# A fused 3x3 convolution and 2x2 max pool: a written-out issue order for its first and last steps, seven weight blocks from six vector operations, three row differences on GpSimd, the last step in halves

## The chip, the cores and the metric

The kernel runs on one core of one Trainium2 chip. The metric is the device time of one execution in microseconds (us). Engines are called PE (TensorE), DVE (VectorE), ACT (ScalarE), POOL (GpSimd) and SP (SyncE, which issues most DMAs here).

## The reference

```python
x = np.random.randn(16, 64, 64, 64)          # batch, channels in, height, width
weight = np.random.randn(128, 64, 3, 3) * 0.1
x_pad = np.pad(x, ((0, 0), (0, 0), (1, 1), (1, 1)))
conv[b, co] += weight[co, ci, kh, kw] * x_pad[b, ci, kh:kh+h, kw:kw+w]   # over ci, kh, kw
output[b, c, i, j] = np.max(conv[b, c, 2*i:2*i+2, 2*j:2*j+2])           # 16 x 128 x 32 x 32
```

## The kernel before, in words

Two images at a time stand on the 128 partitions (64 channels each). The 16 images are eight such pairs. Pairs alternate between two ways of computing: "k" pairs, whose input is a bf16 tile `kx`, and "w" pairs, whose input is an fp32 tile `wx`. A pair's 32 output rows are cut into 4 quarters of 8 rows. One **step** i (0 to 15) handles one quarter of one k pair and the same quarter of one w pair.

The pooling maximum over two neighbouring rows is taken before all products are added: max(a + c, b + c) = max(a, b) + c. So a step builds two PSUM accumulators for the k quarter and two for the w quarter. Each accumulator is a tile of 128 x 2 x 8 x 64 fp32 (the two images side by side); there are four in PSUM. The pieces of a step, with the names that the text uses (upper case for k, lower case for w; the kernel before has the same pieces as functions):

- **PA**: 12 matmuls (`pa`) into the first k accumulator, with weight blocks D2 and G0. **EV** (`evac`): ACT copies it to SBUF.
- **PB**: 12 matmuls (`pb`) into the second k accumulator, with blocks D0 and G2. **MX** (`rowmax`): DVE takes the maximum of it and the copy. **PR**: 6 matmuls (`pr`) add the common part, block G1 times `ks`.
- **OD** (`odd`): ACT copies the odd columns. **CM** (`colmax`): DVE takes the maximum of even and odd columns into `o`, and SP sends `o` out.
- **P2**: 6 matmuls (`p2`) into the first w accumulator, block GM times `we`. **SE** (`se`): ACT writes its negative into the second one. **P0** and **P3** (6 matmuls each) add products of row differences to the first and to the second. **ev**, **mx**, **P1** (6 matmuls, GP times `ws`), **od** and **cm** then do for w what EV, MX, PR, OD and CM do for k.
- The row sums and differences: **KS** (`prep_ks`, bf16) and **WS** (`prep_ws`, fp32) run on DVE, **E** (`prep_we`) on POOL (on DVE for step 0). **Z** (`prep_wz`) is one POOL operation that takes differences two rows apart for all 16 rows of a quarter; P0 reads its even rows and P3 its odd rows.

A step is thus 54 matmuls, all from the helper `taps` (line 159): 864 in all. The 64-partition halves of the array work on the two images at the same time.

Before the steps the weights are loaded (`wraw`), combined into eight blocks `wq` of three kernel columns each (D2 = g2 - g1, D0 = g0 - g1, G0, G1, G2, NG2 = -g2, GM and GP = (g0 + g2 -/+ g1) / 2), transposed on PE (`turn`) and copied back to `wt`. The first rows of the first k pair come as fp32 (`kfirst`) and are cast on DVE in two halves, odd rows (line 301) and even rows (line 311). All other `kx` rows come by DMAs that POOL issues (`kload`), all `wx` rows by DMAs of SP (`wload`). `dummy` issues matmuls on zeros.

The program's order is fixed by hand (`manual_schedule`): each engine takes its instructions in the order in which the code issues them. Lines 291 to 332 are the head; the loop at line 343 issues the pieces of step i mixed with those of step i - 1. `behind(a, b)` makes POOL operation `a` wait for DVE operation `b`:

```python
def behind(inst, other):
    tc.add_manual_dep(inst.ins, other.ins.name, SYNC, reason="shared SBUF port")
...
if i == 0:
    behind(prep_we(1, nc.gpsimd), prep_ws(0))
    prep_wz(1)
preps(i + 1)
```

Of the kernel before, what the change touches and what calls it, by code (L numbers as in the profile page):

```python
# [11 lines left out]
def kernel(  # L12
# [19 lines left out]

    nc = tc.nc
# [5 lines left out]
    MULT = mybir.AluOpType.mult  # L39
# [9 lines left out]
    LEADW = 4  # L49
# [23 lines left out]


# [6 lines left out]
    kfirst = const.tile([128, 2 * R + 1, W], FP32, name="kfirst")  # L81
    nc.sync.dma_start(out=kfirst, in_=rows_of(0, *chunk(0)))

    def kload(j, lo, hi):
        if j not in kx:
            kx[j] = kx_pool.tile([128, H, W], BF16, name="kx")
        nc.gpsimd.dma_start(out=kx[j][:, lo:hi, :], in_=rows_of(2 * j, lo, hi))  # L87
# [5 lines left out]

    for i in range(LEADW):
        wload(i)
# [5 lines left out]
    kload(0, *chunk(1))  # L101
# [5 lines left out]
    D2, G0, D0, G2, GM, NG2, G1, GP = range(0, 24, 3)  # L107
    wv = wraw.rearrange("a (ci k) -> a k ci", k=K * K)
    g0, g1, g2 = wv[:, 0:3, :], wv[:, 3:6, :], wv[:, 6:9, :]
    wq = const.tile([CO, 26, CI], BF16)  # L110
    wt = const.tile([128, 25, CO], BF16)
    nc.vector.memset(wq[:, 0, :], 0.0)
    nc.vector.memset(wq[:, 25, :], 0.0)
    gsum = const.tile([CO, 3, CI], FP32)
    ghalf = const.tile([CO, 3, CI], FP32)

    def dummy(n, tiles):
        for i in range(n):
            yt = tiles[(i // 2) % len(tiles)]
            nc.tensor.matmul(  # L120
                yt[:, i % 2], zeros[:, 0:128], zeros, start=True, stop=True, skip_group_check=True
            )

    tbank = [acc[t][:, h] for t in (1, 2, 2, 3) for h in range(2)]
    tcount = [0]

    def slots(m):
        return wq[:, m + 1 : m + 4, :]  # L130

    def turn(m, engine):
        tp = tbank[tcount[0]].rearrange("p a b -> p (a b)").bitcast(BF16)
        tcount[0] += 1
        n = 4 if m == GP else 3
        for j in range(n):
            nc.tensor.transpose(  # L137
                tp[:, j * 128 : (j + 1) * 128],
                wq[:, m + j : m + j + 2, :].rearrange("a b c -> a (b c)"),
                ident,  # L140
            )
        dst = wt[:, m : m + n, :].rearrange("p a b -> p (a b)")
        if engine is nc.scalar:
            nc.scalar.copy(out=dst, in_=tp[:, 0 : n * 128])  # L144
        else:
            engine.tensor_copy(out=dst, in_=tp[:, 0 : n * 128])  # L146


    def taps(dst, m0, rows, start=False, skip=None):
        for kw in (1, 0, 2):  # L150
            i0, i1 = 0, R
            if skip == 0:
                i0 = 1
            if skip == R - 1:
                i1 = R - 1
            o0, o1, c0, c1 = (0, W, 0, W) if kw == 1 else (1, W, 0, W - 1) if kw == 0 else (0, W - 1, 1, W)
            for half in range(2):
                lo = half * CI
                nc.tensor.matmul(  # L159
                    dst[:, half, i0:i1, o0:o1],  # L160
                    wt[lo : lo + CI, m0 + kw + 1 - half, :],
                    rows(lo, i0, i1, c0, c1),
                    start=start and kw == 1,
                    stop=True,
                    skip_group_check=True,
                )

    def step1(t, first):
# [7 lines left out]


    SYNC = mybir.DependencyInfo(mybir.DependencyClass.Sync, mybir.DependencyReason.DATA)

    def behind(inst, other):  # L180
        tc.add_manual_dep(inst.ins, other.ins.name, SYNC, reason="shared SBUF port")

    ks, ws, we, wz = {}, {}, {}, {}

    def prep_ks(i):
        j, q = divmod(i, NQ)
        if q == 0:
            ks[j] = ks_pool.tile([128, HO, W], BF16, name="ks")
        v = kx[j][:, 2 * R * q : 2 * R * (q + 1), :]
        return nc.vector.tensor_tensor(  # L190
            out=ks[j][:, q * R : (q + 1) * R, :], in0=v[:, 0::2, :], in1=v[:, 1::2, :], op=ADD
        )

    def prep_ws(i):
        j, q = divmod(i, NQ)
        if q == 0:
            ws[j] = ws_pool.tile([128, HO, W], BF16, name="ws")
        v = wx[j % 2][:, 1 + 2 * R * q : 1 + 2 * R * (q + 1), :]
        return nc.vector.tensor_tensor(  # L199
            out=ws[j][:, q * R : (q + 1) * R, :], in0=v[:, 0::2, :], in1=v[:, 1::2, :], op=ADD  # L200
        )

    def prep_we(i, engine):
        j, q = divmod(i, NQ)
        if q == 0:
            we[j] = we_pool.tile([128, HO, W], BF16, name="we")
        v = wx[j % 2][:, 1 + 2 * R * q : 1 + 2 * R * (q + 1), :]
        return engine.tensor_tensor(  # L208
            out=we[j][:, q * R : (q + 1) * R, :], in0=v[:, 1::2, :], in1=v[:, 0::2, :], op=SUB
        )  # L210

    def prep_wz(i):
        j, q = divmod(i, NQ)
        if q == 0:
            wz[j] = wz_pool.tile([128, H, W], BF16, name="wz")
        a = 2 * R * q
        return nc.gpsimd.tensor_tensor(  # L217
            out=wz[j][:, a : a + 2 * R, :],
            in0=wx[j % 2][:, a : a + 2 * R, :],
            in1=wx[j % 2][:, a + 2 : a + 2 * R + 2, :],  # L220
            op=SUB,
        )
# [24 lines left out]
    def se(i):
        tb["w", i] = free.popleft()
        nc.scalar.mul(tb["w", i], ta["w", i], -1.0)  # L249

    def p0(i):
        j, q = divmod(i, NQ)
        taps(ta["w", i], G0, step2(wz[j], 2 * q * R))

    def p3(i):
        j, q = divmod(i, NQ)
        taps(tb["w", i], NG2, step2(wz[j], 2 * q * R + 1))

    def p1(i):
        j, q = divmod(i, NQ)  # L260
        taps(tb["w", i], GP, step1(ws[j], q * R))

    def evac(*g):
        ev[g] = ev_pool.tile([128, 2, R, W], FP32, name="ev")
        nc.scalar.copy(out=ev[g], in_=ta[g])  # L265
        free.append(ta.pop(g))

    def rowmax(*g):
        t = tb[g]
        nc.vector.tensor_tensor(out=t, in0=t, in1=ev.pop(g), op=MAX)  # L270

    def odd(*g):
        od[g] = od_pool.tile([128, 2, R, WO], FP32, name="od")
        nc.scalar.copy(out=od[g], in_=tb[g][:, :, :, 1::2])  # L274

    def colmax(*g):
        t = tb.pop(g)
        o = o_pool.tile([128, 2, R, WO], FP32, name="o")
        nc.vector.tensor_tensor(out=o, in0=t[:, :, :, 0::2], in1=od.pop(g), op=MAX)  # L279
        free.append(t)  # L280
        j, q = divmod(g[1], NQ)
        p = 2 * j + (g[0] == "w")
        nc.sync.dma_start(
            out=out[2 * p : 2 * p + 2, :, q * R : (q + 1) * R, :].rearrange(
# [3 lines left out]
        )  # L288


    dummy(8, [acc[1], acc[2], acc[0], acc[3]])
    klo, khi = chunk(0)
    nc.vector.tensor_sub(out=slots(D2), in0=g2, in1=g1)
    nc.scalar.copy(out=slots(G0), in_=g0)
    nc.vector.tensor_sub(out=slots(D0), in0=g0, in1=g1)
    nc.scalar.copy(out=slots(G2), in_=g2)
    turn(D2, nc.vector)
    turn(G0, nc.scalar)
    turn(D0, nc.vector)
    nc.scalar.mul(ghalf, g1, 0.5)  # L300
    nc.vector.tensor_copy(out=kx[0][:, 1:khi:2, :], in_=kfirst[:, 1:khi:2, :])  # L301
    turn(G2, nc.scalar)
    dummy(2, [acc[0]])
    nc.vector.tensor_add(out=gsum, in0=g0, in1=g2)
    nc.scalar.mul(slots(NG2), g2, -1.0)
    nc.vector.scalar_tensor_tensor(
# [109 lines left out]
```

## Time and profile before

| | us |
|---|---|
| median of 3 timed runs (lowest, highest) | 119.13 (117.88, 120.91) |
| the profiled execution: its own time | 118.08 |
| its span, first to last instruction | 116.3 |
| PE, DVE, ACT, POOL busy | 101.9, 84.7, 72.6, 61.6 |
| mean granted TensorE clock | 0.972 |

The span is 1.8 us shorter than the time of the same execution; all positions in the text are microseconds from the span's start. A busy PE only says that matmuls were under way, so the text counts matmuls and the idle time between them. "Idle before, releaser" in a row is the time the engine stood still, and what ended it.

### The profile page before, as it was taken

The page shows a single profiled execution, that of the slowest core. Times are in us where ns is not written, and L with a number is a line of the kernel's source. Part 1 is how long each engine was busy: PE and PEld are TensorE (multiplying, and loading weights), DVE is VectorE, ACT ScalarE, POOL GpSimd, SP SyncE. Part 2 cuts the span into 40 slices and gives each one's busy share as a digit, 9 for nine tenths or more (in the row PEclk, how much of TensorE's full clock was granted, in tenths as well). Part 3 has the DMA queues.
Part 4 walks back from the last instruction along what each step waited for, and adds up shares of the span by engine and source line. Part 5 has one row for each costly group of instructions (what it writes and reads, how often), then busy time and mean ns, then how long its engine had stood idle before and what let it go on. Part 6 is the DMA issues. An engine that isn't in the chain of part 4 may idle for free.

```text
span 116.3 us, 2320 instructions
## 1 busy us (share of the span) xinstructions
PE 101.9 (88%) x901; PEld 49.3 (42%) x901; DVE 84.7 (73%) x111; ACT 72.6 (62%) x90; POOL 61.6 (53%) x49
## 2 busy tenths in 40 slices
PE   5787974699999999999999999999999999999120
PEld 2333331245455554544555445454554545455000
DVE  1464799758787878787878787878787878787520
ACT  4465338036768676767686767676867676768320
POOL 6000499855656585856386767663965656500000
PEclk9999999679999999999999999999999999999995
DMA  3999129988869488999894799997949422222222
GB/s 99 280 314 368 44 27 186 231 201 145 255 225 208 162 204 146 229 262 253 311 263 148 217 149 263 217 272 286 269 145 208 152 85 93 90 98 88 99 81 90
DMA packets 12459, 21.70 MB, mean 187 GB/s; under 512 B 928, under 2 KB 9120, under 8 KB 12448
## 3 DMA queue, kind: packets, MB, share of 16 engines
q1 hardware_dynamic: 11296, 17.63, 46.9%
q0 software_dynamic: 1152, 3.92, 21.7%
q8 instruction: 7, 0.11, 0.5%
q14 instruction: 4, 0.03, 0.1%
HBM read 17.07 MB, written 8.39 MB: 219 GB/s over the span
## 4 chain that ended last, share of the span: by engine, by line
PE 79%; DVE 10%; DMA 5%; ACT 1%; issue 1%; SPq 0%; DVEq 0%
PE acc L159 78%; DVE ws L199 5%; DMA kfirst<-in_x_dram 5%; DVE acc L270 2%; DVE o L279 1%; PE acc L137 1%; ACT od L274 1%; DVE wt L146 1%; DVE ks L190 1%; ACT wt L144 0%; DVE kx L301 0%; SPq L69 0%; DVEq L146 0%
## 5 line engine op out<-in xcount | busy, mean ns | idle before, releaser
L159 PEld LDWEIGHTS <-wt 64*128 64x128 bf16 x864 | 46.5, 95 | 54.7 <-issue 10.0
L159 PE MATMUL acc<-kx,wt 64*128 64x504 bf16 (+3 forms) x384 | 47.7, 381 | 2.9 <-DVE o L279 2.6
L270 DVE TENSOR_TENSOR acc<-acc,ev 128x1024 f32<-128x1024 f32 x32 | 39.3, 1227 | 13.1 <-PE acc L159 13.1
L217 POOL TENSOR_TENSOR wz<-wx 128x1024 bf16<-128x1024 f32 x16 | 37.7, 2354 | 10.7 <-DVE ks L190 10.7
L265 ACT COPY ev<-acc 128x1024 f32<-128x1024 f32 x32 | 32.4, 1013 | 12.6 <-PE acc L159 11.7
L208 POOL TENSOR_TENSOR we<-wx 128x512 bf16<-128x512 f32 x15 | 19.1, 1272 | 27.5 <-DVE ws L199 21.4
L274 ACT COPY od<-acc 128x512 f32<-128x512 f32 x32 | 18.7, 585 | 19.3 <-PE acc L159 19.3
L279 DVE TENSOR_TENSOR o<-acc,od 128x512 f32<-128x512 f32 x32 | 22.1, 691 | 7.5 <-ACT od L274 7.5
L159 PE MATMUL acc<-wz,wt 64*128 64x504 bf16 (+1 forms) x192 | 23.6, 377 | 0.7 <-POOL wz L217 0.7
L249 ACT ACTIVATE acc<-acc 128x1024 f32<-128x1024 f32 x16 | 16.1, 1008 | 2.2 <-PE acc L120 1.8
L199 DVE TENSOR_TENSOR ws<-wx 128x512 bf16<-128x512 f32 x16 | 16.0, 997 | 0.0
L159 PE MATMUL acc<-ws,wt 64*128 64x504 bf16 (+1 forms) x96 | 13.4, 382 | 2.5 <-DVE acc L270 2.5
L159 PE MATMUL acc<-we,wt 64*128 64x504 bf16 (+1 forms) x96 | 13.2, 377 | 0.2 <-POOL we L208 0.2
L159 PE MATMUL acc<-ks,wt 64*128 64x504 bf16 (+1 forms) x96 | 13.2, 377 | 0.0
L190 DVE TENSOR_TENSOR ks<-kx 128x512 bf16<-128x512 bf16 x16 | 6.6, 414 | 0.0
L120 PE MATMUL acc<-zeros 128*128 128x512 bf16 x12 | 4.5, 517 | 1.2 <-DVE zeros L98 1.2
L87 POOL DMA_DIRECT2D kx<-in_x_dram x8 | 4.7, 584 | 0.1
L137 PE MATMUL acc<-ident,wq 128*128 128x128 bf16 x25 | 2.6, 219 | 2.0 <-DVE wt L146 1.4
L146 DVE COPY wt<-acc 128x384 bf16<-128x384 bf16 (+1 forms) x4 | 1.5, 374 | 3.4 <-PE acc L137 3.4
L144 ACT COPY wt<-acc 128x384 bf16<-128x384 bf16 x4 | 1.9, 478 | 2.9 <-PE acc L137 2.9
L137 PEld LDWEIGHTS <-wq 128*128 128x128 bf16 x25 | 1.6, 97 | 3.7 <-issue 2.9
L120 PEld LDWEIGHTS <-zeros 128*128 128x128 bf16 x12 | 1.3, 126 | 3.3 <-issue 2.1
(25 smaller groups left out, 9.8 us busy)
## 6 DMA issues: line engine op xcount, KB each, us to landing
out_dram<-o SPq DMA_DIRECT2D x32, 256.0 KB, 3.4
wx<-in_x_dram SPq DMA_DIRECT2D x8, 512.0 KB, 6.8
wx<-in_x_dram SPq DMA_DIRECT2D x4, 544.0 KB, 8.9
kx<-in_x_dram POOLq DMA_DIRECT2D x4, 496.0 KB, 8.0
wx<-in_x_dram SPq DMA_DIRECT2D x4, 480.0 KB, 4.8
kx<-in_x_dram POOLq DMA_DIRECT2D x3, 528.0 KB, 9.1
kfirst<-in_x_dram SPq DMA_DIRECT2D x1, 544.0 KB, 5.4
wraw<-in_weight_dram SPq DMA_DIRECT2D x1, 288.0 KB, 3.0
```

The source lines that it names most:

```text
L120: nc.tensor.matmul(yt[:, i % 2], zeros[:, 0:128], zeros, start=True, stop=True, skip_group_check=True)
L137: nc.tensor.transpose(tp[:, j * 128 : (j + 1) * 128], wq[:, m + j : m + j + 2, :].rearrange("a b c -> a (b c)"), ident,)
L159: nc.tensor.matmul(dst[:, half, i0:i1, o0:o1], wt[lo : lo + CI, m0 + kw + 1 - half, :], rows(lo, i0, i1, c0, c1), start=start and kw == 1, ...
L190: return nc.vector.tensor_tensor(out=ks[j][:, q * R : (q + 1) * R, :], in0=v[:, 0::2, :], in1=v[:, 1::2, :], op=ADD)
L199: return nc.vector.tensor_tensor(out=ws[j][:, q * R : (q + 1) * R, :], in0=v[:, 0::2, :], in1=v[:, 1::2, :], op=ADD)
L208: return engine.tensor_tensor(out=we[j][:, q * R : (q + 1) * R, :], in0=v[:, 1::2, :], in1=v[:, 0::2, :], op=SUB)
L217: return nc.gpsimd.tensor_tensor(out=wz[j][:, a : a + 2 * R, :], in0=wx[j % 2][:, a : a + 2 * R, :], in1=wx[j % 2][:, a + 2 : a + 2 * R + ...
L249: nc.scalar.mul(tb["w", i], ta["w", i], -1.0)
L265: nc.scalar.copy(out=ev[g], in_=ta[g])
L270: nc.vector.tensor_tensor(out=t, in0=t, in1=ev.pop(g), op=MAX)
L274: nc.scalar.copy(out=od[g], in_=tb[g][:, :, :, 1::2])
L279: nc.vector.tensor_tensor(out=o, in0=t[:, :, :, 0::2], in1=od.pop(g), op=MAX)
```

## The change

Six things change. (1) The order of all pieces is written out as a list of names: `HEAD` (steps 0 to 3), `STEADY` (steps 4 to 12, the same order each time) and `TAIL` (steps 13 to 15). (2) Seven weight blocks take the place of eight: NG2 goes, and the halving of GM and GP moves into the copies out of PSUM. One ACT copy writes G0, G1 and G2; D2, D0, GM, GP are DVE operations and g0 + g2 one on POOL; each takes its elements in another order than before. (3) Z is split: `wz` for P0 and `wy` (**Y**) for P3, each 8 rows, so that a step has three POOL operations of 128 x 512 elements in place of one of that size and one of twice that. Every POOL operation waits for the last DVE operation on SBUF tiles that the list names before it. (4) The four zero matmuls in the head outside the warm-up of eight go; two are issued where the first SE needs a PSUM tile in a defined state. (5) The first `kload` waits for the sixth warm-up matmul; the later ones are issued behind Y.0, and behind Y of the third and fourth quarter. (6) EV, MX, ev, mx, OD, CM, od and cm of step 15 are done for one image at a time (".0", ".1"), and their output goes out in four DMAs of half the size.

```diff
-    D2, G0, D0, G2, GM, NG2, G1, GP = range(0, 24, 3)
+    G0, G1, G2, D2, D0, GM, GP = 1, 4, 7, 11, 15, 19, 23
...
+    def on_vector(inst):
+        sbuf_op[0] = inst
+        return inst
+    def on_gpsimd(inst):
+        behind(inst, sbuf_op[0])
+        return inst
...
+    def turn_out(m):
...
+        if m == "GM":
+            nc.scalar.mul(dst, src, 0.5)
+        elif m == "GP":
+            nc.vector.tensor_scalar_mul(out=dst, in0=src, scalar1=0.5)
...
-        taps(tb["w", i], NG2, step2(wz[j], 2 * q * R + 1))
+        taps(tb["w", i], G2, step1(row["wy", i // NQ], i % NQ))
...
+    def wz(i):
+        on_gpsimd(row_op(nc.gpsimd, "wz", i, -1, 1, SUB))
+    def wy(i):
+        on_gpsimd(row_op(nc.gpsimd, "wy", i, 2, 0, SUB))
+        j, q = divmod(i, NQ)
+        if i == 0:
+            kload(0, chunk(2)[0], H)
+        if q == 2 and j + 1 < NP // 2:
+            kload(j + 1, 0, H // 2 + 1)
+        if q == 3 and j + 1 < NP // 2:
+            kload(j + 1, H // 2 + 1, H)
...
+    def kernel_rows():
+        nc.scalar.copy(out=wq[:, G0 : G0 + 9, :].rearrange("a k c -> a c k"), in_=wv)
...
+    HEAD = """
+        D2 D0 GS TD2 VD2 GA TG0 VG0 TG1 VG1 TG2 VG2 TD0 XE GM TGM GP TGP XO KS.0 VD0 VGM VGP
+        PA.0 EV.0 Y.0 PB.0 E.0 P2.0 SE.0 MX.0 PA.1 EV.1 PR.0 Z.0 P0.0 P3.0 E.1 WS.0 P2.1 KS.1
+        OD.0 CM.0 PB.1 Z.1 ev.0 WS.2 SE.1 P0.1 ev.1 mx.0 P1.0 od.0 Y.1 P3.1 MX.1 PR.1 OD.1 PA.2
+        E.2 WS.1 KS.2 cm.0 PB.2 CM.1 P2.2 Z.2 mx.1 P1.1 EV.2 MX.2 PR.2 SE.2 od.1 cm.1 OD.2 CM.2
+        Y.2 E.3 Z.3 Y.3 P0.2 P3.2 KS.3 WS.3 PA.3 E.4 ev.2 mx.2 P2.3 EV.3 Z.4 PB.3 SE.3 Y.4 MX.3
+        P1.2 od.2 cm.2 P0.3 P3.3 ev.3 PR.3 KS.4 WS.4
+    """
+    STEADY = """
+        PA+0 OD-1 E+1 CM-1 P2+0 mx-1 EV+0 Z+1 PB+0 SE+0 Y+1 P1-1 MX+0 P0+0 od-1 P3+0 cm-1 ev+0
+        PR+0 KS+1 WS+1
+    """
+    TAIL = """
...
+        mx.14 Y.15 Z.15 EV.15.0 EV.15.1 PB.15 MX.15.1 MX.15.0 SE.15 P0.15 P3.15 ev.15.0 mx.15.0
+        ev.15.1 mx.15.1 P1.14 od.14 cm.14 PR.15 OD.15.1 OD.15.0 CM.15.0 CM.15.1 P1.15 od.15.0
+        cm.15.0 od.15.1 cm.15.1
+    """
...
+    for n in range(8):
+        warm = zero(n // 2, n % 2)
+        if n == 5:
+            behind(kload(0, *chunk(1)), warm)
```

In `HEAD`, "T" before a block's name is its transposes, "V" its copy out of PSUM; GA is `kernel_rows`, GS is g0 + g2 on POOL, XE and XO are the casts of even and odd rows of `kfirst`.

What this does to the instruction order at three places. First DVE in the head, from the second cast on, before (`acc_88` to `acc_90` are PSUM accumulators; line 146 copies a transposed block out of PSUM, 208 is E, 190 KS, 270 MX, 199 WS, 279 CM):

```order
L311 CAST kx<-kfirst 128x9x64
L146 COPY wt<-acc_89 128x384
L314 SCALAR_TENSOR_TENSOR wq<-gsum,ghalf 128x192
L208 TENSOR_TENSOR we<-wx_93 128x512
L146 COPY wt<-acc_90 128x512
L190 TENSOR_TENSOR ks<-kx 128x512
L270 TENSOR_TENSOR acc_88<-acc_88,ev 128x1024
L199 TENSOR_TENSOR ws<-wx_93 128x512
L190 TENSOR_TENSOR ks<-kx 128x512
L199 TENSOR_TENSOR ws<-wx_93 128x512
L279 TENSOR_TENSOR o<-acc_88,od 128x512
L270 TENSOR_TENSOR acc_90<-acc_90,ev 128x1024
```

The same place on DVE after the change (line 335 is a cast, 354 and 357 are GM and GP, 247 is every row sum or difference, 166 and 162 copy out of PSUM, 298 is MX, 317 CM):

```order
L335 CAST kx<-kfirst 128x9x64
L354 TENSOR_TENSOR wq<-gsum,wraw 128x64x3
L357 TENSOR_TENSOR wq<-gsum,wraw 128x64x3
L335 CAST kx<-kfirst 128x8x64
L247 TENSOR_TENSOR ks<-kx 128x512
L166 COPY wt<-acc_78 128x512
L162 TENSOR_SCALAR wt<-acc_80 128x512
L247 TENSOR_TENSOR we<-wx_82 128x512
L298 TENSOR_TENSOR acc_78<-acc_78,ev 128x1024
L247 TENSOR_TENSOR ws<-wx_82 128x512
L247 TENSOR_TENSOR ks<-kx 128x512
L317 TENSOR_TENSOR o<-acc_78,od 128x512
```

The second WS no longer stands between KS.1 and the first CM; GM and GP now stand between the two casts, ahead of the odd rows that PA.0 reads.

Second, POOL in the head, before (217 is Z, 87 issues a `kx` load):

```order
L217 TENSOR_TENSOR wz<-wx_93 128x1024
L87 DMA kx<-in_x_dram 128x1984
L87 DMA kx<-in_x_dram 128x2112
L208 TENSOR_TENSOR we<-wx_93 128x512
L217 TENSOR_TENSOR wz<-wx_93 128x1024
```

and after (345 is GS, 95 issues a `kx` load):

```order
L95 DMA kx<-in_x_dram 128x1024
L345 TENSOR_TENSOR gsum<-wraw 128x64x3
L247 TENSOR_TENSOR wy<-wx_82 128x512
L95 DMA kx<-in_x_dram 128x1984
L247 TENSOR_TENSOR wz<-wx_82 128x512
L247 TENSOR_TENSOR we<-wx_82 128x512
```

The first difference of step 0 moved ahead of the load of the later rows, and one load for the second k pair left this place.

Third, the end of DVE's program, before:

```order
L279 TENSOR_TENSOR o<-acc_88,od 128x512
L270 TENSOR_TENSOR acc_90<-acc_90,ev 128x1024
L270 TENSOR_TENSOR acc_88<-acc_88,ev 128x1024
L279 TENSOR_TENSOR o<-acc_90,od 128x512
L279 TENSOR_TENSOR o<-acc_88,od 128x512
L270 TENSOR_TENSOR acc_87<-acc_87,ev 128x1024
L279 TENSOR_TENSOR o<-acc_87,od 128x512
```

and after:

```order
L298 TENSOR_TENSOR acc_81<-acc_81,ev 128x1024
L298 TENSOR_TENSOR acc_78<-acc_78,ev 128x512 x2
L298 TENSOR_TENSOR acc_79<-acc_79,ev 128x512 x2
L317 TENSOR_TENSOR o<-acc_81,od 128x512
L317 TENSOR_TENSOR o<-acc_78,od 128x256 x2
L317 TENSOR_TENSOR o<-acc_79,od 128x256 x2
```

The last mx (on `acc_87` before, on `acc_79` after) stood behind CM.15 and stands ahead of it now, in two halves.

388 lines of the change are left out of this document (179 added, 209 removed).

## The prediction

> **What bounds the kernel now.** I read the shares of the chain that ended last first, then that chain in order of time, then the two places where it leaves PE. The shares by engine:
>
> ```profile
> PE 79%; DVE 10%; DMA 5%; ACT 1%; issue 1%; SPq 0%; DVEq 0%
> ```
>
> PE carries it, so the question is where PE is not fed. The chain (start, length, what):
>
> ```profile
> 1.19 5.44 DMA kfirst<-in_x_dram
> ...
> 6.65 0.44 DVE kx L301
> ...
> 7.13 1.39 PE acc L159 x12
> ...
> 14.28 1.90 DVE ws L199
> 16.18 0.34 DVE ks L190
> 16.51 4.33 DVE ws L199
> 20.84 0.61 DVE o L279
> ...
> 21.49 86.67 PE acc L159 x792
> ...
> 109.41 1.23 DVE acc L270
> ...
> 110.69 0.84 PE acc L159 x6
> ...
> 111.55 0.59 ACT od L274
> ...
> 112.16 0.69 DVE o L279
> ```
>
> There are three parts. From 7.13 to 21.49 the chain runs over DVE (WS, KS, WS, CM); of the 864 matmuls only 864 - 792 - 6 = 66 are done by then. From 21.49 to 108.16 PE runs 792 without a hole. Then it waits 2.5 us for mx, runs the last 6 and leaves copy, maximum and write to the end. The middle is PE's own rate, as one matmul group of two successive steps shows (PA.5 and PA.6):
>
> ```profile
> 44.19 1.47 PE L159 MATMUL acc<-kx,wt 64*128 64x512 bf16 x12
> ...
> 50.02 1.47 PE L159 MATMUL acc<-kx,wt 64*128 64x512 bf16 x12
> ```
>
> 5.83 us for 54 matmuls is 0.108 us each, and 864 of them take **93.3 us**. The first tap starts at 7.13 and the last ends at 111.53, so holes in between are 111.53 - 7.13 - 93.3 = **11.1 us**. From 111.53 to the end of the span are 4.8 us: 1.3 of copy and maximum, 3.45 of the last write from 112.85 on. The kernel after has the same 864 taps of the same shapes, so I predict three things: when the first tap starts, the holes, and the end.
>
> **Why there are holes.** DVE and POOL in the worst stretch, and PE behind it:
>
> ```profile
> 16.44 4.41 DVE L199 TENSOR_TENSOR ws<-wx 128x512 bf16<-128x512 f32 x1
> 16.69 1.29 POOL L208 TENSOR_TENSOR we<-wx 128x512 bf16<-128x512 f32 x1
> ...
> 17.92 2.36 POOL L217 TENSOR_TENSOR wz<-wx 128x1024 bf16<-128x1024 f32 x1
> ...
> 21.49 2.74 PE L159 MATMUL acc<-kx,wt 64*128 64x512 bf16 x12 [2.63 <-DVE o L279]
> ```
>
> The view of the tile `ws` has the durations of WS (least, median, most, in ns):
>
> ```profile
> L199 DVE TENSOR_TENSOR ws<-wx x16: 682/683/4405, 14.2 to 102.0; 128x512 bf16<-128x512 f32 x16
> ```
>
> A WS that takes 0.68 at its median takes 4.41 and ends 0.6 us after POOL's two operations: it makes no way while POOL reads the same SBUF. CM.0 stands behind it, PB.1 waits for CM.0's accumulator. The stall also cost the clock (columns: window, length, busy PE, PEld, DVE, ACT, POOL, granted clock, DMA share, GB/s):
>
> ```profile
> 21.00:22.00 1.00, 0.51 (x4) 0.25 (x5) 1.00 (x2) 0.00 (x0) 1.00 (x1) 0.54 1.06 215
> 22.00:23.00 1.00, 1.00 (x8) 0.39 (x6) 0.58 (x1) 0.00 (x0) 1.00 (x2) 0.50 0.94 246
> ...
> 24.00:25.00 1.00, 1.00 (x10) 0.52 (x8) 0.67 (x1) 0.00 (x0) 1.00 (x2) 0.76 0.85 231
> ```
>
> After 2.6 us without matmuls (18.9 to 21.5) PE runs at half clock until about 24.5, some 1.5 us of work lost (the 12 taps at 21.49 took 2.74, against 1.47).
>
> **The change part by part.** Durations that I use:
>
> ```profile
> L270 DVE TENSOR_TENSOR acc<-acc,ev 128x1024 f32<-128x1024 f32 x32 | 39.3, 1227 | 13.1 <-PE acc L159 13.1
> L217 POOL TENSOR_TENSOR wz<-wx 128x1024 bf16<-128x1024 f32 x16 | 37.7, 2354 | 10.7 <-DVE ks L190 10.7
> ...
> L208 POOL TENSOR_TENSOR we<-wx 128x512 bf16<-128x512 f32 x15 | 19.1, 1272 | 27.5 <-DVE ws L199 21.4
> ...
> L279 DVE TENSOR_TENSOR o<-acc,od 128x512 f32<-128x512 f32 x32 | 22.1, 691 | 7.5 <-ACT od L274 7.5
> ...
> L190 DVE TENSOR_TENSOR ks<-kx 128x512 bf16<-128x512 bf16 x16 | 6.6, 414 | 0.0
> ...
> L87 POOL DMA_DIRECT2D kx<-in_x_dram x8 | 4.7, 584 | 0.1
> ...
> L296 ACT CAST wq<-wraw 128x192 bf16<-128x192 f32 x1 | 0.5, 533 | 0.0
> ...
> L293 DVE TENSOR_TENSOR wq<-wraw 128x192 bf16<-128x192 f32 x1 | 0.5, 501 | 2.6 <-DMA wraw<-in_weight_dram 2.6
> ...
> L311 DVE CAST kx<-kfirst 128x576 bf16<-128x576 f32 x1 | 0.5, 484 | 0.0
> L301 DVE CAST kx<-kfirst 128x512 bf16<-128x512 f32 x1 | 0.4, 428 | 0.6 <-DMA kfirst<-in_x_dram 0.6
> ...
> L306 DVE SCALAR_TENSOR_TENSOR wq<-gsum,ghalf 128x192 bf16<-128x192 f32 x1 | 0.4, 359 | 0.1
> ```
>
> *First tap, later by 1.3 us.* PA.0 now needs XE, GM, GP and XO behind each other on DVE, from `kfirst` landing at 6.6 (chain above): 0.48 + 0.50 + 0.50 + 0.43, less about 0.05 overlap at each start, ends at 8.4; PA.0 starts at 8.45 instead of 7.13. GM and GP in the new element order are not in the trace. Below, 0.36 each (line 306, contiguous); above, 0.68 (a WS of 512 elements), so -0.3 to +0.35; I take line 293, which also reads strided weights. The other head operations have cover. GA on ACT costs between 0.53 (one block, line 296) and three times that, from 3.8 on; PE needs it only before TGM at 7.6, so even 1.6 is hidden under the wait for `kfirst`. GS on POOL is bounded by 1.3 (a whole E), starts at 4.8 behind D0 and is wanted at 7.1. The six small memsets come before the weights land. One transpose more and two zero matmuls (0.43) count in the holes.
>
> *Head, holes of about 0.6 us instead of 8.* With those rows I follow the list in order, each engine in turn, PE at 0.108 per tap. PE: PA.0 8.45, PB.0 9.8, P2.0 11.1 (E.0 is done at 10.8, behind Y.0 on POOL), zeros, PA.1 12.1. DVE: MX.0 ends 12.5; WS.0 waits under E.1 on POOL and ends 13.9; KS.1 14.3; CM.0 15.9, because OD.0 waits for PR.0. PB.1 starts at 16.0, where it was 21.5. So the long wait goes, since the second WS (WS.2 now) stands behind CM.0 and POOL's next operation waits for it. What is late next are the margins: PB.1 against CM.0 0.1 us, P0.1 against SE.1 (17.3) 0.05, P1.0 against mx.0 0.25, PR.1 against MX.1 0.35; PR.2 waits 0.2 for MX.2 (24.0). PA.3 starts at 26.0, and KS.3 waits until 26.9 under Z.3 and Y.3, with mx.2 done just before P1.2 at 29.2. By PR.3's end at **31.9**, 210 taps are done; before, that was 21.49 + 144 x 0.108 + 1.5 = 38.5.
>
> *The loads that moved:*
>
> ```profile
> kx<-in_x_dram POOLq DMA_DIRECT2D x3, 528.0 KB, 9.1
> ...
> kx<-in_x_dram POOLq DMA_DIRECT2D x1, 256.0 KB, 9.1
> ```
>
> The first `kload` is issued at 3.9 instead of 1.4; another 9.1 us gives 13.0, and PA.1 wants it at 12.1. A shorter queue of `wx` ahead of it gives less; I take no wait, with 0.9 as the far end. The load of the later rows stands behind Y.0 (10.1) for PA.2 at 19.9: covered. The first load of pair 2 is issued behind Y.2 at 22.6 and lands at 31.7 by the upper row, where PA.4 wants it at 31.8: no wait, up to 1 us if slower.
>
> *Steps 4 to 12, nothing.* PE's, DVE's and ACT's orders are those of the loop before. A WS and the KS that follows it:
>
> ```profile
> 49.84 0.68 DVE L199 TENSOR_TENSOR ws<-wx 128x512 bf16<-128x512 f32 x1
> ...
> 55.35 0.41 DVE L190 TENSOR_TENSOR ks<-kx 128x512 bf16<-128x512 bf16 x1
> ```
>
> POOL pays 3 x 1.27 = 3.8 instead of 1.27 + 2.35 = 3.6 for a step, from the end of WS on; with a load to issue (0.58) it ends 4.4 after, and KS comes 55.35 - 50.52 = 4.8 after. That margin of 0.4 us hides it; without it KS would be held as WS was.
>
> *End.* mx.15 in halves (0.69 each) stands ahead of CM.15. mx.14 ends 99.6, MX.15 101.0 and mx.15 102.3; P1.15 waits 0.3 and ends at 103.1, where PE waited 2.5 before. Then DVE has cm.14 (until 103.0) and four half maxima (0.42 each), the last at **104.6**. The last write, half the size, I take at 3.2 (2.9 to 3.45). The span is **107.8**: 8.45 + 93.3 + 1.3 of holes (zeros 0.43, head 0.3, mx.14 to P1.15 0.6) + 1.5 + 3.2.
>
> The profiled execution took 118.08 with a span of 116.3, so 1.8 more: 109.6. Its time is 1.05 below the median of the runs shown, so against that median I say **110.6**.
>
> **The rivals.**
>
> *A, the clock falls in the head.* After warm-up at 4.5, PE has only transposes until 8.45. In the stretch above 2.6 us of idling sufficed. If it falls, up to 3.4 us run at half clock (21.1 to 24.5 in the windows): 1.5 us, and the time is 112.1. Against it: before, PE idled for much of 4.5 to 7.1 and kept its clock, with one thing between that now goes, two matmuls on zeros:
>
> ```profile
> 6.23 0.59 PE L120 MATMUL acc<-zeros 128*128 128x512 bf16 x2
> ```
>
>  The Trainium skill, "TensorE: Matmul & The Clock Gate" (Part 4: PE-mode transpose), says that transposes don't count as PE being busy; by that rule the whole 4 us are idle and this rival is the forecast. This trace doesn't settle that, for those two matmuls.
>
> Chance of A: 0.18.
>
> *B, margins and loads slip.* `kx` lands late for PA.1 (0.9) or PA.4 (1.0), or POOL's operations and DVE's chain eat the margins of 0.05 to 0.35: 1 to 3 us in all, 111.6 to 113.6. For it: nearly every hand-over in the head is tight, and waits on one engine pass to the next. Chance 0.18.
>
> *C, the change doesn't free the head.* A DVE operation starves behind POOL again (WS.0 or KS.3): 3.7 us as at 16.44, and 1.5 of clock, 115.8. The Trainium skill, "SBUF — State Buffer" (Who interferes with whom), says that whoever issues first keeps the shared port; here the trace differs, WS issued first (16.44 against 16.69) and lost, POOL taking its usual 1.29. By the page the order written here would be safer, and I would give this half the chance. Against it: most POOL operations now wait for DVE. Chance 0.05.
>
> *D, slower: POOL becomes the bound of the steady steps.* A step needs POOL's three differences and, apart from them, KS and WS: 3x + 1.2. That reaches 5.83 at x = 1.54 per operation, and eats the whole gain at x = 1.8; at 2.35, each costing what the old Z did, a step is 8.25, and 12 steps add 29: 140. At 1.9 it is 6.9, +12.8: 123.4. Against it: E has the same shape and the same stride of rows and takes 1272 ns in the mean of 15 operations, and Z's 2.35 is for twice the elements. Chance 0.03.
>
> **How the numbers follow.** The forecast (109.3 to 111.3) has 0.56, A 0.18, B 0.18, C 0.05, D 0.03. The range goes from 108.7 (GM and GP short, `kfirst` early, the write at 2.9) to 113.8, the top of B; it leaves out C, D and A with B together. The runs before spread by 2.5%, so 2% (2.4 us) is about what a measurement tells from no change. Faster by over 2% means under 116.7: all but D and a little of C and B, 0.94; same 0.03, slower 0.03.
>
> **What would show it.** In the profile after: the first tap near 8.5; no WS or KS over 2 us; no PE idling over 0.5 us between 8.5 and 103; a steady step still at 5.83; POOL operations near 1.27; PE's last tap less than 0.5 us after mx.15.1; the clock at 1.0 from 4 us on. Wrong would make it: a granted clock of 0.5 around 8 to 12 (A), a wait of PE's weight loads on a `kx` DMA (B), a step over 6 us (D).

## The result and the profile after

| | median us (lowest to highest) | runs |
|---|---|---|
| before | 118.86 (117.88 to 120.91) | 4 |
| after | 110.83 (110.30 to 111.25) | 4 |

The ratio of the two is 0.9348, with a 95% interval from 0.9261 to 0.9434: 6.5% faster. The profiled execution took 111.17 with a span of 109.4; before, these were 118.08 and 116.3. The forecast was 110.6, and 107.8 for the span. (Ratios leave out executions of 1.5% or more above the fastest of the same kernel, and from the profiled executions of b3, a3 and a4, which are such, only short durations and the order are read.)

The chain of the changed kernel, first its shares by engine, then in order of time (start, length, what):

```profile
PE 84%; DVE 6%; DMA 5%; issue 1%; ACT 1%; SPq 0%; DVEq 0%
```

```profile
1.18 5.22 DMA kfirst<-in_x_dram
...
6.42 0.49 DVE kx L335
6.92 0.92 DVE wq L354
7.84 0.87 DVE wq L357
...
8.75 0.61 PE acc L147 x4
9.36 3.79 PE acc L182 x30
...
24.31 1.24 DVE acc L298
...
25.59 69.08 PE acc L182 x642
...
105.81 0.42 DVE o L317
```

WS, KS and CM have left the head of the chain, and from 9.36 on it is PE with short visits to DVE. What the change costs stands ahead of that: GM (line 354) and GP (357) lie between the cast of the even rows and the first tap. Places to hold against before (start, length, engine, line, operation, names, shape, count, and the idle time before with what ended it):

```profile
9.29 3.21 PE L182 MATMUL acc<-kx,wt 64*128 64x512 bf16 x24
...
17.27 0.68 DVE L247 TENSOR_TENSOR ws<-wx 128x512 bf16<-128x512 f32 x1
17.52 1.46 PE L182 MATMUL acc<-kx,wt 64*128 64x512 bf16 x12
...
32.64 0.83 PE L182 MATMUL acc<-ks,wt 64*128 64x512 bf16 x6
...
85.41 1.48 PE L182 MATMUL acc<-kx,wt 64*128 64x512 bf16 x12
...
91.24 1.04 PE L182 MATMUL acc<-kx,wt 64*128 64x512 bf16 x8
...
103.68 0.83 PE L182 MATMUL acc<-ws,wt 64*128 64x512 bf16 x6 [0.39 <-DVE acc L298]
...
105.40 0.37 ACT L303 COPY od<-acc 128x256 f32<-128x256 f32 x1 [0.49 <-DVE o L317]
105.81 0.42 DVE L317 TENSOR_TENSOR o<-acc,od 128x256 f32<-128x256 f32 x1 [0.44 <-ACT od L303]
```

PB.1 starts at 17.52 (before: 21.49), and the second WS to be issued takes 0.68 (before: 4.41). Step 13, the first of `TAIL`, still takes 91.24 - 85.41 = 5.83, and so does step 5 of the steady loop (from 39.05 to 44.88 in the trace). PE waits 0.39 for the last mx, where it waited 2.5. By the prediction's own count:

| us | before | after | forecast |
|---|---|---|---|
| first tap | 7.13 | 9.29 | 8.45 |
| holes | 11.1 | 104.51 - 9.29 - 93.3 = 1.9 | 1.3 |
| last tap to the end of the span | 4.8 | 4.9 | 4.7 |
| span | 116.3 | 109.4 | 107.8 |

The span is 6.9 shorter: 9.2 of holes are gone, 2.16 are given back before the first tap, 0.1 at the end. The groups of DVE and POOL (count, busy time, mean ns, idle before):

```profile
L247 POOL TENSOR_TENSOR we<-wx 128x512 bf16<-128x512 f32 x15 | 19.0, 1269 | 18.3 <-DVE ws L247 10.9
...
L247 POOL TENSOR_TENSOR wz<-wx 128x512 bf16<-128x512 f32 x16 | 20.3, 1270 | 4.0 <-DVE ws L247 1.9
L247 DVE TENSOR_TENSOR ws<-wx 128x512 bf16<-128x512 f32 x16 | 11.2, 700 | 0.0
L247 DVE TENSOR_TENSOR ks<-kx 128x512 bf16<-128x512 bf16 x16 | 7.9, 492 | 0.0
```

Half of the old Z takes 1.27, as E does. The mean of WS is 700 ns and its longest takes 911, so none is starved; KS has risen from 414 to 492 ns in the mean, and its longest from 415 to 984: some of them still wait a little under POOL.

### The profile page after: what moved, and what is told of

It is laid out like the page before. It is cut to its first block, busy times and chain, and to the rows that moved or that the text cites. A ratio compares the mean times of both kernels' runs of the same rounds, so it can differ in the third digit from the quotient of the medians.

```text
span 109.4 us, 2345 instructions
## 1 busy us (share of the span) xinstructions
PE 101.5 (93%) x900; PEld 51.8 (47%) x900; DVE 83.5 (76%) x117; ACT 73.2 (67%) x90; POOL 64.6 (59%) x66
## 4 chain that ended last, share of the span: by engine, by line
PE 84%; DVE 6%; DMA 5%; issue 1%; ACT 1%; SPq 0%; DVEq 0%
PE acc L182 83%; DMA kfirst<-in_x_dram 5%; DVE acc L298 2%; DVE o L317 2%; DVE wq L354 1%; DVE wq L357 1%; ACT od L303 1%; PE acc L147 1%; PE acc L134 0%; DVE kx L335 0%; SPq L103 0%; DVEq L317 0%; DVEq L298 0%
## 5 line engine op out<-in xcount | busy, mean ns | idle before, releaser
L298 DVE TENSOR_TENSOR acc<-acc,ev 128x1024 f32<-128x1024 f32 (+1 forms) x34 | 39.4, 1165 | 12.0 <-PE acc L182 9.9
L285 ACT COPY ev<-acc 128x1024 f32<-128x1024 f32 (+1 forms) x34 | 32.5, 963 | 15.1 <-PE acc L182 13.5
L317 DVE TENSOR_TENSOR o<-acc,od 128x512 f32<-128x512 f32 (+1 forms) x34 | 22.1, 658 | 7.0 <-ACT od L303 6.4
L303 ACT COPY od<-acc 128x512 f32<-128x512 f32 (+1 forms) x34 | 19.0, 561 | 11.2 <-PE acc L182 10.0
L247 POOL TENSOR_TENSOR wy<-wx 128x512 bf16<-128x512 f32 x16 | 20.3, 1270 | 8.9 <-DVE ws L247 5.8
L247 POOL TENSOR_TENSOR wz<-wx 128x512 bf16<-128x512 f32 x16 | 20.3, 1270 | 4.0 <-DVE ws L247 1.9
L182 PE MATMUL acc<-wz,wt 64*128 64x504 bf16 (+1 forms) x96 | 13.2, 377 | 0.0
L182 PE MATMUL acc<-wy,wt 64*128 64x504 bf16 (+1 forms) x96 | 13.2, 377 | 0.0
L247 DVE TENSOR_TENSOR ws<-wx 128x512 bf16<-128x512 f32 x16 | 11.2, 700 | 0.0
L339 ACT CAST wq<-wraw 128x576 bf16<-128x576 f32 x1 | 2.8, 2787 | 1.7 <-DMA wraw<-in_weight_dram 1.7
```

Of the source, the lines that this page charges most:

```text
L182: nc.tensor.matmul(dst[:, half, i0:i1, o0:o1], wt[lo : lo + CI, m0 + kw - half, :], rows(lo, i0, i1, c0, c1), start=start and kw == 1, sto ...
L247: return engine.tensor_tensor(out=row_out(name, i), in0=row_in(t, f + a, pad), in1=row_in(t, f + b, pad), op=op)
L285: nc.scalar.copy(out=ev[g][:, halves(h)], in_=acc[ta[g]][:, halves(h)])
L298: nc.vector.tensor_tensor(out=t, in0=t, in1=ev[g][:, halves(h)], op=MAX)
L303: nc.scalar.copy(out=od[g][:, halves(h)], in_=acc[tb[g]][:, halves(h), :, 1::2])
L317: nc.vector.tensor_tensor(out=o, in0=acc[tb[g]][:, s, :, 0::2], in1=od[g][:, s], op=MAX)
```

## The experiments

My theory: the gain is the starved WS in the head and mx.15's place at the end. The rivals: the gain is the head's order as a whole, or the split of Z, or the halves at the end, with A (clock) and D (POOL) as losses that are still there. The names b are edits of the kernel before, a of the kernel after. Ratios are to the kernel before, run beside them, with 95% intervals.

**b1, one wait moved.** In the kernel before, POOL's differences of step 1 wait until the second WS is done, where E.1 waited for the first one only; those of step 2 waited for the second one already.

```diff
             if i == 0:
-                behind(prep_we(1, nc.gpsimd), prep_ws(0))
+                prep_ws(0)
+                prep_ks(1)
+                last = prep_ws(1)
+                behind(prep_we(1, nc.gpsimd), last)
                 prep_wz(1)
-            preps(i + 1)
+                behind(prep_we(2, nc.gpsimd), last)
+                prep_wz(2)
+            else:
+                preps(i + 1)
```

> The kernel before with one edit: POOL's differences of steps 1 and 2 wait until DVE has done WS.1, instead of starting while it is at work. Theory (the head of the kernel before is lost because WS.1 starves while POOL reads the same SBUF): WS.1 takes 0.7 instead of 4.4, CM.0 comes near 19.1, PB.1 near 19.2 instead of 21.5, PE never idles long enough to lose its clock: 2.3 + 1.5 = 3.7 us less, ratio to before 0.97. Rival (WS.1 is slow for another reason, a late wx load for instance): WS.1 stays over 2 us, ratio 1.00.

Measured: 115.84, ratio 0.9706 (0.9646 to 0.9767), so 3.5 us (2.8 to 4.2). The tile `ws` (least, median, most in ns) and the place of the stall:

```profile
L199 DVE TENSOR_TENSOR ws<-wx x16: 677/684/1989, 14.5 to 99.5; 128x512 bf16<-128x512 f32 x16
```

```profile
16.79 0.68 DVE L199 TENSOR_TENSOR ws<-wx 128x512 bf16<-128x512 f32 x1
17.55 1.26 POOL L208 TENSOR_TENSOR we<-wx 128x512 bf16<-128x512 f32 x1 [0.52 <-DVE ws L199]
...
19.55 1.47 PE L159 MATMUL acc<-kx,wt 64*128 64x512 bf16 x12
```

The WS of 4.4 us is gone, though no work has been taken away. (The 1989 ns is the first WS, at 14.54, under Z.0; the kernel before has it too, and in the changed kernel this WS takes 0.76.) PB.1 starts 1.9 us sooner, and its 12 taps take 1.47 where they took 2.74: the stall had cost the clock as well.

**b2, mx.15 ahead of CM.15** in the kernel before.

```diff
-        if i:
+        if i and i < N:
             rowmax("w", i - 1)
...
             preps(i + 1)
+            if i == N - 1:
+                rowmax("w", i)
             odd("k", i)
```

> The kernel before with one edit: in the last step mx.15 stands ahead of CM.15 on DVE. Theory (PE waited 2.5 us at the end only because mx.15 stood behind CM.15): mx.15 starts when ev.15 is done (107.9), ends at 109.1, P1.15 starts there instead of at 110.7: 1.5 us less, ratio 0.987. The rest of the 2.5 us, ACT's copy ev.15 and mx.15 itself, stays. Rival (mx.15 waits for something else): no change, 1.00.

Measured: 117.09, ratio 0.9822 (0.9778 to 0.9867), 2.1 us (1.6 to 2.6). PE's wait for the last mx:

```profile
109.86 0.82 PE L159 MATMUL acc<-ws,wt 64*128 64x512 bf16 x6 [1.07 <-DVE acc L270]
```

It falls from 2.5 to 1.07, the 1.5 us that were expected; the runs give 0.6 more than the trace explains. Added up, b1 and b2 are 5.6 us, where the ratio of the whole change is worth 7.7 (6.6 in a0, below); no run has both edits. What is left I did not separate. The rest of the head's order, the first WS among it, would have to make it up, net of the later first tap; that is not shown.

**b3, Z in two operations of 8 rows** in the kernel before.

```diff
-        return nc.gpsimd.tensor_tensor(
-            out=wz[j][:, a : a + 2 * R, :],
...
+        for s in range(2):
+            inst = nc.gpsimd.tensor_tensor(
+                out=wz[j][:, a + s : a + s + 2 * R - 1 : 2, :],
...
```

> The kernel before with one edit: Z of 16 rows becomes two POOL operations of 8 rows each (even and odd rows), in the same place. Theory (an operation of 8 rows costs what E costs, and POOL has room): 2 x 1.27 in place of 2.35, the steady step stays at 5.83, the time within 0.5 us of before, ratio 1.00. Rival (operations with every other row cost what the long one did): 2 x 2.35, POOL needs 6 us and the two sums of DVE another 1.1, the step grows to about 7.2 and the time by 15 us or more.

Measured: 119.93, ratio 1.0041 (0.9995 to 1.0087). POOL's group:

```profile
L218 POOL TENSOR_TENSOR wz<-wx 128x512 bf16<-128x512 f32 x32 | 40.5, 1287 | 11.0 <-DVE ks L190 11.0
```

Two of 1.29 instead of one of 2.35: the split by itself gains nothing, and costs 1.0 us at most by the interval. (Here the two still write alternate rows of one tile; in the change each has its own.)

**a1, a fourth POOL difference** of the same size in each of steps 5 to 12, into a tile that nothing reads: rival D pushed until it should bind.

```diff
...
+        if FIRST < i <= LAST:
+            nc.gpsimd.tensor_tensor(
+                out=spare, in0=row_in(wx[j % 2], 2 * R * q + 2, 1), in1=row_in(wx[j % 2], 2 * R * q, 1), op=SUB
+            )
```

> The changed kernel with one addition: in steps 5 to 12 POOL does one more difference of the same size behind Y (into a tile that nothing reads). It measures how far POOL is from being the bound. Theory (a step costs POOL and DVE's two sums together, 4 x 1.25 + 1.2 = 6.2, and 0.6 more where a load is issued, since a sum on DVE waits while POOL is at work): steps of 6.2 to 6.8 instead of 5.83, 8 of them, so 3 to 6 us longer than the changed kernel's 110.8: 114 to 117, with KS and WS stretched. Rival (POOL and the two sums run beside each other): 4 x 1.25 + 0.6 = 5.6 is still under 5.83, and the time stays at 111.

Measured: 111.97, ratio 0.9405 (0.9352 to 0.9457). The interval overlaps that of the changed kernel, and the 3 to 6 us of my law did not come. PE in two successive steps, a KS that is held, and the tile `ks`:

```profile
51.33 1.48 PE L182 MATMUL acc<-kx,wt 64*128 64x512 bf16 x12
...
56.59 1.08 DVE L249 TENSOR_TENSOR ks<-kx 128x512 bf16<-128x512 bf16 x1
...
57.09 1.40 PE L182 MATMUL acc<-kx,wt 64*128 64x512 bf16 x12
```

```profile
L249 DVE TENSOR_TENSOR ks<-kx x16: 411/716/1423, 8.8 to 91.9; 128x512 bf16<-128x512 bf16 x16
```

KS does wait under POOL now (0.72 at the median instead of 0.41), so the mechanism is real, but PE's step does not grow: the one shown (step 7, whose PB leaves out a row at the border) takes 57.09 - 51.33 = 5.76, and 56.47 - 50.72 = 5.75 in the changed kernel. From PA.4 to PA.10 the two traces take 68.74 - 33.91 = 34.83 and 68.06 - 33.29 = 34.77. The law 3x + 1.2 left out that late sums meet slack. POOL is not the bound of the steady steps, not with four operations either.

**a0, the changed kernel again**, unedited, beside a2 to a4 on the same chip.

> The changed kernel itself, as the mark for the three kernels beside it: 110.8, ratio to before 0.935. All theories expect the same.

Measured: 111.69, ratio 0.9446 (0.9363 to 0.9528). In its profile the first 24 taps and two windows (columns as in the prediction; the clock is third from the end):

```profile
9.02 4.02 PE L182 MATMUL acc<-kx,wt 64*128 64x512 bf16 x24
```

```profile
8.00:9.00 1.00, 0.54 (x5) 0.34 (x4) 0.97 (x3) 0.83 (x2) 0.00 (x0) 0.67 1.10 356
9.00:10.00 1.00, 1.00 (x7) 0.44 (x8) 1.00 (x4) 0.00 (x0) 0.79 (x1) 0.50 1.12 278
```

At full clock these taps take 2.69 (a5, below), so 1.3 us are lost: nearly the 1.5 of rival A. The changed kernel's first profile lost 0.5 in another way: PE reached full clock only during the first taps (3.21 for 24). Its windows show a clock of 1.00 there, but its weight transposes took 310 ns in the mean, where at full clock they take 219 (before, and a6, below). The same 24 taps took 4.04 in a1, 3.39 in a2, 4.20 in a3 and 3.28 in a7, so every profile with this head lost between 0.5 and 1.5 us.

**a2, step 15 in one piece.**

```diff
-        mx.14 Y.15 Z.15 EV.15.0 EV.15.1 PB.15 MX.15.1 MX.15.0 SE.15 P0.15 P3.15 ev.15.0 mx.15.0
-        ev.15.1 mx.15.1 P1.14 od.14 cm.14 PR.15 OD.15.1 OD.15.0 CM.15.0 CM.15.1 P1.15 od.15.0
-        cm.15.0 od.15.1 cm.15.1
+        mx.14 Y.15 Z.15 EV.15 PB.15 MX.15 SE.15 P0.15 P3.15 ev.15 mx.15
+        P1.14 od.14 cm.14 PR.15 OD.15 CM.15 P1.15 od.15 cm.15
```

> The changed kernel with the last step's copies and maxima in one piece instead of halves, in the same order. Theory (the halves bring next to nothing: after P1.15 the two copies and two maxima of 0.37 and 0.42 and the smaller write take 4.9 us, and one copy of 0.59, one maximum of 0.69 and a write of 3.45 take 4.8): within 0.3 us of the changed kernel. Rival (the halves hide copies under maxima, as intended by any such split, and the smaller write lands sooner): 0.8 us slower or more.

Measured: 111.21, ratio 0.9419 (0.9343 to 0.9495): the halves bring nothing that can be measured. In its trace the last mx's wait is the same, and from the start of P1.15 to the last maximum's end it is even shorter, 105.96 + 0.69 - 104.48 = 2.17 against 106.23 - 103.68 = 2.55 with halves:

```profile
104.48 0.83 PE L182 MATMUL acc<-ws,wt 64*128 64x512 bf16 x6 [0.42 <-DVE acc L298]
...
105.96 0.69 DVE L317 TENSOR_TENSOR o<-acc,od 128x512 f32<-128x512 f32 x1 [0.34 <-ACT od L303]
```

The halves win most of it back at the write: 109.4 - 106.23 = 3.17 for the last, against 110.1 - 106.65 = 3.45 for the whole one.

**a3, both last copies ahead of the maxima.**

```diff
-        cm.15.0 od.15.1 cm.15.1
+        od.15.1 cm.15.0 cm.15.1
```

> The changed kernel with the order of the last four pieces od.15.0, od.15.1, cm.15.0, cm.15.1 instead of od.15.0, cm.15.0, od.15.1, cm.15.1. In the trace od.15.1 starts only when cm.15.0 has ended (105.40), though the two touch different halves. Theory (the wait comes with the order in the list, and goes with it): od.15.1 follows od.15.0 at once, cm.15.1 ends 0.45 us sooner, time 0.4 us less. Rival (the copy waits for the maximum in any order): no change.

Measured: 111.74, ratio 0.9371 (0.9273 to 0.947): not to be told from the changed kernel by time. In the trace the copies now follow each other:

```profile
106.53 0.65 ACT L303 COPY od<-acc 128x256 f32<-128x256 f32 x2 [0.57 <-DVE o L317]
107.20 0.76 DVE L317 TENSOR_TENSOR o<-acc,od 128x256 f32<-128x256 f32 x2 [0.34 <-ACT od L303]
```

From the first copy's start to the last maximum's end it is 1.43, against 106.23 - 104.54 = 1.69 in the changed kernel. So in the changed kernel the second copy's wait of 0.49 on the first maximum follows the order of the list. Why two different columns of the same tile order each other at all stays open.

**a4, the weight blocks in the element order of before**: contiguous writes, strided reads.

```diff
-    wv = wraw.rearrange("a (c k) -> a c k", k=K * K)
-    g0, g1, g2 = wv[:, :, 0:3], wv[:, :, 3:6], wv[:, :, 6:9]
+    wv = wraw.rearrange("a (c k) -> a k c", k=K * K)
+    g0, g1, g2 = wv[:, 0:3, :], wv[:, 3:6, :], wv[:, 6:9, :]
...
```

> The changed kernel with the six weight operations in the element order of the kernel before (reads with a stride of 9 elements, writes side by side) instead of reads side by side and bf16 writes 64 elements apart. Theory (the scattered writes made GM and GP 0.9 each, D2 and D0 about 1 and the one copy GA 2.8): GM and GP 0.36 to 0.5, GA 1.3 to 1.6, the first tap at 8.4 to 8.6 instead of 9.3, time 0.8 us less. Rival (three blocks from one read of fp32 weights are slow in any order): the same durations, no change. A third way (the first tap is earlier but PE then waits for the kx load of PA.1 or at CM.0): half of the gain or less.

Measured: 110.54, ratio 0.934 (0.9259 to 0.9421). The groups of a4 and then of the changed kernel:

```profile
L339 ACT CAST wq<-wraw 128x576 bf16<-128x576 f32 x1 | 1.2, 1222 | 1.7 <-DMA wraw<-in_weight_dram 1.7
...
L354 DVE TENSOR_TENSOR wq<-gsum,wraw 128x192 bf16<-128x192 f32 x1 | 0.5, 482 | 0.0
```

```profile
L339 ACT CAST wq<-wraw 128x576 bf16<-128x576 f32 x1 | 2.8, 2787 | 1.7 <-DMA wraw<-in_weight_dram 1.7
...
L354 DVE TENSOR_TENSOR wq<-gsum,wraw 128x192 bf16<-128x192 f32 x1 | 1.0, 1007 | 0.0
```

The new element order doubles these operations on DVE and ACT: 0.48 against 1.01, 1.22 against 2.79. The edit turns round the order of writes and of reads together, and with it the length of the inner run (64 elements, or 3 and 9); a4 doesn't separate these. Its head shows what the order costs the first tap:

```profile
7.37 0.49 DVE L335 CAST kx<-kfirst 128x576 bf16<-128x576 f32 x1 [1.70 <-DMA kfirst<-in_x_dram]
...
9.07 4.33 PE L182 MATMUL acc<-kx,wt 64*128 64x512 bf16 x24
```

From the cast's start to the first tap it is 9.07 - 7.37 = 1.70, against 9.29 - 6.42 = 2.87 in the changed kernel. In this execution `kfirst` landed 0.95 later, so the first tap comes hardly sooner, and its taps run at half clock. Whether the 0.8 us that were expected arrive can't be seen from the times: the interval overlaps those of the changed kernel (0.9261 to 0.9434 and 0.9363 to 0.9528).

**a5, a4 and four zero matmuls** ahead of the transposes of GM, to keep PE busy.

```diff
-        ... TG2 VG2 TD0 XE GM TGM GP TGP XO KS.0 VD0 VGM VGP
+        ... TG2 VG2 TD0 F.1 F.2 F.3 F.3 XE GM TGM GP TGP XO KS.0 VD0 VGM VGP
...
```

> The changed kernel with the weight operations in the old element order, and with four matmuls on zeros in PE's program between the transposes of D0 and those of GM, where PE waits for the kfirst cast. Theory (PE runs the first taps at half clock because little but transposes comes between the warm-up and the first tap): the granted clock is 1.0 at the first tap, the first 24 taps take 2.7 to 3.0 instead of 3.2 to 4.3, and the time is 0.5 to 1.5 us below the kernel with the old element order alone (110.5). Rival (the clock falls whatever PE does there, or is not the reason): no change, or 0.3 longer by the matmuls added.

Measured: 109.72, ratio 0.9298 (0.9226 to 0.937). The first taps, and what comes next:

```profile
7.82 2.69 PE L182 MATMUL acc<-kx,wt 64*128 64x512 bf16 x24
...
12.95 1.25 PE L182 MATMUL acc<-kx,wt 64*128 64x512 bf16 x10 [1.25 <-DMA kx<-in_x_dram]
```

The first tap comes 1.5 us sooner than in the changed kernel, at full clock. Of that, 0.84 is the cast, which starts at 5.58 instead of 6.42; from the cast to the first tap it is 2.24 (a4: 1.70, without the four matmuls). Then PA.1 waits 1.25 us for the first `kload`: rival B's load, hidden as long as the head was slow. This supports the clock theory: a4 differs by the four matmuls only and took 4.33 for these taps, and a8, below, has the matmuls and takes 2.69 again. How much time the four are worth isn't settled, since a4's interval overlaps.

**a6, a warm-up of 40 transposes of zeros** instead of the 8 zero matmuls. It asks whether transposes count as work for the clock, the point that the prediction left open at rival A.

```diff
-    for n in range(8):
-        warm = zero(n // 2, n % 2)
+    for n in range(40):
+        warm = nc.tensor.transpose(
+            acc[n // 10][:, 0].rearrange("p a b -> p (a b)").bitcast(BF16)[:, 0:128], zeros[:, 0:128], ident
+        )
...
```

> The changed kernel with 40 transposes of zeros in place of its warm-up of eight matmuls on zeros; PE then has nothing but transposes until the first tap. It asks whether transposes raise and keep PE's clock. Theory T1 (they count as work): the clock is at full speed before the first tap, at 4 to 8 us, as after the warm-up before; the first taps take 377 ns. Theory T2 (they don't count): the first taps take 600 ns, and full speed comes only after some 2 to 3.4 us of taps, at 11 us or later; the time is then 1 to 2 us longer than with T1.

One execution: 110.28, span 108.5. Its warm-up transposes, its weight transposes and its first taps:

```profile
L395 PE MATMUL acc<-ident,zeros x40: 219/314/314, 1.4 to 5.5; 128*128 128x128 bf16 x40
...
L147 PE MATMUL acc<-ident,wq x26: 219/219/230, 5.5 to 8.8; 128*128 128x128 bf16 x26
```

```profile
8.94 2.69 PE L182 MATMUL acc<-kx,wt 64*128 64x512 bf16 x24
```

With nothing but transposes before, a transpose falls from 314 to 219 ns, and the first 24 taps take 2.69: full clock. Here transposes do count. The Trainium skill, "TensorE: Matmul & The Clock Gate" (Part 4: PE-mode transpose), says that they don't count as PE being busy in the same way; this run differs, and the measurement decides.

**a7, eight output buffers instead of four.** In a0 a CM waited for the write that had its output buffer, and PE 0.65 for this CM. The view of waits of a0 (what waited for what: us in total, times, longest):

```profile
DVE o L317 <- DMA out_dram<-o: 1.2, 1, 1.2
```

```diff
-    o_pool = ctx.enter_context(tc.tile_pool(name="o_pool", bufs=4))
+    o_pool = ctx.enter_context(tc.tile_pool(name="o_pool", bufs=8))
```

> The changed kernel with eight output buffers instead of four. In several traces of the changed kernel CM waits 0.5 to 1.6 us once for a write from an output buffer that took about 12 us to land. Theory (that wait comes through to PE, whose accumulator CM frees): the wait goes, and the time falls by 0.3 to 1.2 us. Rival (PE has slack there, or the write would hold up something else): no change.

Measured: 111.36, ratio 0.9409 (0.9333 to 0.9485): no gain. The wait is gone from its trace, and another one stands in the chain:

```profile
84.67 1.45 DVE ks L247
```

A KS is held 1.45 under Y: now and then the margin of 0.4 in a middle step is used up in the changed kernel's order too, with three POOL operations only. POOL's E came late there. The row in a7, and then the view of waits of the changed kernel:

```profile
82.12 1.27 POOL L247 TENSOR_TENSOR we<-wx 128x512 bf16<-128x512 f32 x1 [3.96 <-DVE acc L298]
```

```profile
POOL we L247 <- DMA wx<-in_x_dram: 6.6, 2, 3.5
```

In the changed kernel the same E waits 3.50 for a `wx` load, and the next KS takes 0.98. That a7's E waited for this load too is likely, but its row names DVE.

**a8, a3 + a5 + a7 in one kernel.**

> All together: the old element order of the weight operations, the four matmuls on zeros, eight output buffers, and od.15.1 ahead of cm.15.0. If the terms add up (0.8 + 1.0 + 0.5 + 0.4 from the changed kernel's 111.2 in the mean of its runs): 108.5, ratio to before 0.915. If they cover each other: 110.

Measured: 109.63, ratio 0.9298 (0.9238 to 0.9358), the same as a5: the parts don't add up. It beats the kernel before by 7.0%. The changed kernel's two measurements lie 0.6 us (0.9348) and 1.8 us (0.9446) above it; the interval of the first overlaps with a8's, that of the second does not. It is the fastest version here, by a margin that these runs don't fix.

## Why the prediction was right, and where it was not

**The bound and the main mechanism were right.** Three of its points are shown, not argued: one wait moved in the kernel before brings 3.5 us (b1), the order of two DVE operations at the end 1.5 us by its trace and 2.1 by the runs (b2), and the split of Z nothing (b3). The rest, 2.1 us of the 7.7 (1.0 of the 6.6 in a0), is not separated. The middle kept its 5.83 per step. After PR.3 the forecast was exact: from 31.9 to 103.1 is 71.2; from 33.29, where PR.3's matmuls give way to PA.4's, to 104.51, the end of the last tap (103.68 + 0.83), it is 71.2 too.

**The step that failed is "First tap, later by 1.3 us".** Measured were 2.16. GM and GP were taken at 0.50 each, with 0.68 as the upper end; on the chain they took 0.92 and 0.87, 0.79 more together, outside of the bound. I bounded them by rows with contiguous writes and took line 293 because it reads strided weights; a4 shows that the element order decides (0.48 and 0.50 in the old one), and with it the stretch from the cast to the first tap is 1.70, where the forecast had 8.45 - 6.6 = 1.85. The Trainium skill, "SBUF — State Buffer" (the note on 16-byte cachelines in Door 1), says that each access that crosses to a new line pays; the blocks' writes lie 64 bf16 elements apart, and the doubled durations agree. By itself this doesn't say why a4's reads, 9 fp32 elements apart, cost so little. GA, by the same error, took 2.79 and not at most 1.6; in the profiles of a2 and a7 the chain starts with it instead of `kfirst`, and in a3 with the two DVE operations D2 and D0. `kfirst` landed 0.2 sooner, and the four transposes of GP at half clock delayed the first tap more than the second cast did.

**Rival A was given 0.18, and a part of it happened in every profile of the changed head**: 0.5 us in its own, 1.3 in a0. "The clock at 1.0 from 4 us on" was wrong, and the sum put this loss at nothing. My argument against it, PE idling before without loss, did not carry. The kernel before, b1, b2 and b3 all took 1.39 for their first 12 taps, which is full clock. What had gone with the change were the two matmuls on zeros ahead of the first tap; with four in their place (a5, a8) nothing is lost, and in a4, without them, 1.6 us are. Why a6 loses nothing without them stays open.

With the first tap (0.84) and the clock (0.5), PR.3 ends at 33.29 instead of 31.9; the other holes of the head together are as large as the walk through the list had them. A further 0.2 at the end is the wait of the second copy (a3); the last write took 3.17, where 3.2 was forecast. Together that is the 1.6 by which the span was forecast too short.

**The median was hit so closely by luck, through a second error.** I added 1.05, because the kernel before was profiled in an execution that was faster than its median. The changed kernel was profiled in one 0.34 above its median (111.17 against 110.83). Too short by 1.6 and too long by 1.4 leaves 0.2. The range held each single error. (Its upper end of 113.8 is called the top of B, which the text puts at 113.6.)

**B and D.** No load holds up PE in the changed kernel's profile, but POOL waits twice for a `wx` load (6.6 us in all, the longest 3.5), which no rival had; B's `kload` shows only in a5, and not in a8, where the head is nearly as fast. D's price was several times too high (a1), and only an occasional KS is held (0.98 in the changed kernel, 1.45 in a7). C did not happen. Of the halves the forecast had 0.25 for a shorter last write: it came (0.28), and was lost to the second copy's wait (a2).

## What to carry to other kernels

When an operation takes six times its median, look at what the other engine does in the same microseconds: moving one wait, with the same work, was worth 3.5 us here. Price an operation by a row with the same access pattern on the write side as well as on the read side; where no such row exists, the bound must be wide: twice the nearest row was needed here. A head has several bounds behind each other (weights, clock, first loads), so ask of each gain what is late next, and expect gains there not to add up.

## What the runs showed of the hardware

With bf16 writes that lie 64 elements apart an operation took twice as long as with writes side by side: 1.01 against 0.48 us for 192 elements on DVE (the changed kernel against a4), 2.79 against 1.22 for 576 on ACT; the order of the reads changed with it. Transposes alone brought PE to full clock (a6, one execution: 314 to 219 ns). The clock's steps fall at other places from one execution of the same kernel to the next (3.21 and 4.02 for the same 24 taps). What makes it fall in the head is open: before, 2.6 us without matmuls sufficed, and in a0 it fell at 8.3 (0.67 granted from 8 to 9), after PE was busy for 0.23, 0.45 and 0.89 of the three microseconds from 5 to 8. A DVE sum that met POOL operations following each other made next to no way until they were done (4.41 us before, 0.68 in b1); which of the two started first did not decide it (16.44 for DVE's, 16.69 for POOL's).
